# A hybrid decoder trunk on one core: the scan's decays made in two steps, and the last layer's roots moved from GpSimd to ScalarE and VectorE

## The chip, the cores and the metric

One core of a Trainium2 chip runs the whole program. Its engines are TensorE (PE, with its weight loads as PEld), VectorE (DVE), ScalarE (ACT), GpSimd (POOL) and SyncE (SP), each with a queue of its own that it works off in order, and DMA engines that move data between the memories. The metric is the device time of one execution in microseconds: 824.66 us before (the median of three runs, 824.23 to 825.6).

## The reference

Two layers (DEPTH = 2) on 256 tokens of 1024 channels in fp32. Each layer normalises the stream by its root mean square, projects it with one large matrix, and feeds three token mixers: a Mamba-2 state space scan (SSD), sliding-window attention, and forgetting attention. Each mixer's output is gated, projected back to 1024 channels, and merged under sigmoid gates; one more projection is added to the stream. After the second layer a last normalisation gives the output. The two parts that matter here:

```python
def rms_norm(x, w):
    xf = x.astype(jnp.float32)
    y = xf * lax.rsqrt(jnp.mean(xf * xf, axis=-1, keepdims=True) + NORM_EPS)
    return (y * w.astype(jnp.float32)).astype(x.dtype)

# in ssd_chunked_scan: two chunks of 128 tokens, 4 groups of 4 heads
    seg = a_cum[..., :, None] - a_cum[..., None, :]
    decay = jnp.where(causal, jnp.exp(jnp.where(causal, seg, 0.0)), 0.0).astype(dtype)
    cb = jnp.einsum('bclgn,bcsgn->bgcls', cc, bc)
    y_diag = jnp.einsum('bgrcls,bcsgrp->bclgrp', cb[:, :, None] * decay, x_dt)
```

## The kernel before

**Weights and matmuls.** All large products are made with split operands. A weight piece is loaded in fp32 (tile `raw`, 128x1024, queue of SP), ScalarE copies it rounded to `hi`, and VectorE subtracts to get `lo` (function `split`, L286 and L287). PE then multiplies high by high, low by high and high by low into one PSUM bank (`mm`, all matmuls stand at L106, transposes at L110). SP's loads run six pieces ahead, the splits up to four parts ahead of the piece in use.

**What sets the order.** PE's instructions are issued in the order in which the program writes them. A list of operations walks through the weight pieces; between them `pump` enters the steps of generators (`ssd_group`, `swa_quad`, `fox_quad` and others) whose due time has come. A generator says with `yield D_...` how many estimated PE microseconds must pass before its next step. For the other engines a scheduler of the framework chooses the order from the dependencies and from where in the program an instruction was written, so that an instruction written later tends to stand later; `pin` keeps an instruction in the program's order, and `tc.high_priority()` moves one ahead.

**The scan.** `ssd_group(y, g)` makes one group of four heads. Its second step builds for each of the two chunks four decay matrices on VectorE (L829, 128x128 each, `dec`), exponentiates all four in one ScalarE activation (L831), then exponentiates the cumulated sums of the second chunk (L835, `cx`) and multiplies them with C on VectorE (L836). It yields `D_SSD` = 8.0; the next step multiplies the decays with the chunk's products (L848), and after that PE uses them. VectorE and ScalarE work at the same time on the convolution units of the branch: a unit's high and low sums are added by a GpSimd-issued transfer (`dma_sum`, L487), then come an activation (L773), three taps on VectorE (L776), a tanh (L782) and a product (L783).

**The end.** In the last layer `u_out2` and `u_out` make the last projection in three column blocks (256, 512, 256) for each of the two token halves. `out_end` adds the residual (L1133), sums squares (on ScalarE, L242, or for the last block on VectorE, L1137), and for the last block makes the variance, one value per partition, and calls `row_rsqrt2`: GpSimd raises it to the power -0.5 (L253), and two VectorE instructions refine it by a Newton step (L255, L257). Then VectorE scales columns 0 to 639 (L1156), ScalarE the rest (L1158), and SP and ScalarE issue the output transfers (L1157, L1159). Rows with line L1510 are the closing instructions of the program: each engine's DRAIN and the barrier's semaphores, in which GpSimd collects the others.

**The activation table.** Exp, Tanh and Abs run under one table, loaded once at the start beside a 1-wide activation on the tile `tab` (L183).

Of the kernel before, what the change touches and what calls it, by code (L numbers as in the profile page):

```python
# [21 lines left out]
NEG = -1.0e30  # L22
EPS = 1e-6

D_SOFT, D_SOFT2, D_EVAC, D_SSD, D_SSD2 = 7.0, 3.0, 3.0, 8.0, 4.0
D_K, D_Q, D_QK, D_G0, D_FOX, D_BDMA, D_BIAS, D_BC, D_SSD3 = 6.0, 5.5, 2.0, 8.0, 0.0, 4.0, 2.6, 5.5, 1.0
D_GN1, D_GN2, D_CUM, D_H, D_M = 8.0, 13.5, 12.0, (4.8, 6.4), 5.0
BUDGET = 1.35
# [19 lines left out]
def hybrid_trunk(  # L48
# [17 lines left out]
    def T(tag, shape, dtype=F32, bufs=None):  # L66
        count[0] += 1
        return sb.tile(shape, dtype, tag=tag, name=f"{tag}_{count[0]}",
                       bufs=bufs if bufs is not None else BUFS.get(tag, 1))
# [92 lines left out]
    def drain(br):  # L162

        left = 0
        while any(m[2] == br for m in waiting):
            for m in sorted(waiting, key=lambda m: (m[0], m[1])):
                if m[2] == br and allowed(m):
                    left += 1
                    enter(m)
                    break  # L170
            else:
                m = min((m for m in waiting if allowed(m)), key=lambda m: (m[0], m[1]))
                left += 1
                enter(m)
        if left and VERBOSE:
            print("drained", br, left, "at", round(clock["t"], 1))
# [70 lines left out]
        ts(v[:, 0:1], v[:, 0:1], 1.0 / D, EPS, op0=ALU.mult, op1=ALU.add)  # L247
        return v

    def row_rsqrt2(v):  # L250

        r0 = T("sm", [P, 8])
        nc.gpsimd.tensor_tensor(r0[:, 0:1], v, mhalf[:, 0:1], op=ALU.pow)  # L253
        a = T("sm", [P, 8])
        stt(a[:, 0:1], r0[:, 0:1], v, r0[:, 0:1], op0=ALU.mult, op1=ALU.mult)  # L255
        r = T("rs", [P, 8], bufs=4)
        stt(r[:, 0:1], a[:, 0:1], -3.0, r0[:, 0:1], op0=ALU.add, op1=ALU.mult)  # L257
        return r
# [21 lines left out]
    def pin(f):  # L280
        return lambda *a, **k: tc.keep_in_program_order(f(*a, **k))  # L281
# [517 lines left out]
    def ssd_group(y, g):  # L799
        yield lambda: not any(m[2] == 1 for m in waiting)  # L800
        yield "bcg"
        bcg = T("L4", [P, 4, S])
        nc.scalar.dma_start(bcg, y.cumd[4 * g:4 * g + 4, 0, :].partition_broadcast(P))
        yield D_BC
        yield "ssd"
        xdt = T("L2", [P, 2, 256])
        hs = slice(4 * g, 4 * g + 4)
        for t in range(2):
            p = pmx()
            for j in range(2):  # L810
                transpose(p[:, j * P:(j + 1) * P], y.xs[:, 2 * g + j, t * P:(t + 1) * P], ident)
            tt(xdt[:, t, :].rearrange("p (h d) -> p h d", h=4),  # L812
               p[:, 0:256].rearrange("p (h d) -> p h d", h=4), bc(y.dt[:, t, hs], 2, 64), op=ALU.mult)
        p = pmx()
        transpose(p[:, 0:P], y.bcT[:, g, 0:P], ident)
        bt = T("bt", [P, P])
        act(bt, p[:, 0:P], AF.Copy)
        ds = T("ds", [P, 4], bufs=2)
        tt(ds, bcg[:, :, P - 1], y.acum[:, 0, hs], op=ALU.subtract)
        act(ds, ds, AF.Exp)  # L820
        xds = T("L1", [P, 256])
        tt(xds.rearrange("p (h d) -> p h d", h=4), xdt[:, 0, :].rearrange("p (h d) -> p h d", h=4),
           bc(ds, 2, 64), op=ALU.mult)
        decs = []
        for c in range(2):
            tk = slice(c * P, (c + 1) * P)
            dec = T("L2", [P, 4, P])
            for h in range(4):
                stt(dec[:, h, :], bcg[:, h, tk], y.acum[:, c, 4 * g + h:4 * g + h + 1], negtri,  # L829
                    op0=ALU.subtract, op1=ALU.add)  # L830
            act(dec, dec, AF.Exp)  # L831
            decs.append(dec)

        cx = T("L2", [P, 4, P])
        act(cx, bcg[:, :, P:S], AF.Exp)  # L835
        tt(cx, cx, bc(y.bcT[:, 4 + g, P:S], 1, 4), op=ALU.mult)  # L836
        yield D_SSD
        tokens["bcg"] += 1

        p = pmx()  # L840
        mm(p[:, 0:256], bt, xds, start=True, stop=True)
        for c in range(2):
            tk = slice(c * P, (c + 1) * P)
            mm(p[:, 256 + c * P:384 + c * P], y.bcT[:, g, tk], y.bcT[:, 4 + g, tk], start=True, stop=True)
        st = T("st", [P, 256])
        act(st, p[:, 0:256], AF.Copy)
        for c in range(2):
            tt(decs[c], decs[c], bc(p[:, 256 + c * P:384 + c * P], 1, 4), op=ALU.mult)  # L848
        yield Half(D_SSD2)

        py = pmx()
        for c in range(2):
            for j in range(2):
                o = py[:, S * j + P * c:S * j + P * c + P]
                for s in range(c + 1):
                    for i in range(2):
                        h = 2 * j + i
                        hc = slice(64 * h, 64 * h + 64)
                        a, b = (xdt[:, c, hc], decs[c][:, h, :]) if s == 0 else (st[:, hc], cx[:, h, :])
                        mm(o[64 * i:64 * i + 64, :], a, b, start=(s == 0), stop=(s == c))  # L860
        for j in range(2):
            u = 2 * g + j
            stt(y.xs[:, u, :], y.xs[:, u, :], y.dsk[:, u:u + 1], py[:, S * j:S * j + S], op0=ALU.mult, op1=ALU.add)
        yield D_SSD3
        tokens["ssd"] += 1
# [233 lines left out]
    def out_start(y, c, t, i, n):  # L1099
        xo = T("L1" if n == 256 else "L2", [P, n])  # L1100
        xsrc = x2 if y.l == 0 else xres
        nc.scalar.dma_start(xo, xsrc[t * P:(t + 1) * P, c:c + n])
        if i == 0:
            y.ss[t] = T("ss", [P, 4], bufs=4)
            if t == 0:
                y.xn = T("L8", [P, 2, D])
        return xo
# [8 lines left out]
    def u_out2(y, c):  # L1116

        def f(w):
            def late():
                drain(8)  # L1120
                limit(None, True)
            drain(7)
            xo = [out_start(y, c, t, 0, w.n) for t in range(2)]
            none = lambda: None
            for t, p in enumerate(tok2(y.mh, y.ml, w, (none, late, none, none))):
                out_end(y, c, t, 0, w.n, xo[t], p)
            state["pin"] = False
        return f

    def out_end(y, c, t, i, n, xo, p):  # L1130
        sl = slice(c, c + n)
        with tc.high_priority():
            tt(halves(y.xn[:, t, sl]), p, halves(xo), op=ALU.add)  # L1133
            last = y.l + 1 == L
            if last and i == 2:
                junk = T("L2", [P, 512])
                nc.vector.tensor_tensor_reduce(out=junk[:, 0:n], in0=y.xn[:, t, sl], in1=y.xn[:, t, sl],  # L1137
                                               scale=1.0, scalar=0.0, op0=ALU.mult, op1=ALU.add,
                                               accum_out=y.ss[t][:, i:i + 1])
            else:  # L1140
                sum_sq(y.xn, t, c, y.ss[t][:, i:i + 1], n)
            nwb = fin["w"] if last else layers[y.l + 1].nwb
            if i == 2:
                v = y.var[t][:, 1:2]
                pin(stt)(v, y.ss[t][:, 2:3], 1.0 / D, y.var[t][:, 0:1], op0=ALU.mult, op1=ALU.add)
            if last:
                pin(stt)(y.xn[:, t, sl], y.xn[:, t, sl], -0.5, nwb[:, sl], op0=ALU.mult, op1=ALU.mult)
            else:
                nc.scalar.dma_start(xres[t * P:(t + 1) * P, sl], y.xn[:, t, sl])
            if i == 1:  # L1150
                y.var[t] = row_var(y.ss[t], 2)
            if i == 2:
                r = row_rsqrt2(v)
                if last:
                    m = 640
                    ts(y.xn[:, t, 0:m], y.xn[:, t, 0:m], r[:, 0:1], None, op0=ALU.mult)  # L1156
                    nc.sync.dma_start(out2[t * P:(t + 1) * P, 0:m], y.xn[:, t, 0:m])  # L1157
                    act(y.xn[:, t, m:D], y.xn[:, t, m:D], AF.Copy, scale=r[:, 0:1])  # L1158
                    nc.scalar.dma_start(out2[t * P:(t + 1) * P, m:D], y.xn[:, t, m:D])  # L1159
                else:  # L1160
                    h = layers[y.l + 1].h[t] = T("L4", [P, D])
                    for j in range(2):
                        hs = slice(j * 512, (j + 1) * 512)
                        stt(h[:, hs], y.xn[:, t, hs], r[:, 0:1], nwb[:, hs], op0=ALU.mult, op1=ALU.mult)
        if i == 2 and not last:
            launch(5 + t, hT(layers[y.l + 1], t), D_H[t])
        if i == 1:
            pump()
# [345 lines left out]
```

## Time and profile before

| | before |
|---|---|
| median of 3 runs | 824.66 us (824.23 to 825.6) |
| the profiled execution's own time | 825.03 us |
| its span (first to last instruction) | 823.0 us, granted clock 0.996 |
| PE / DVE / ACT / POOL busy | 99% / 81% / 67% / 21% |
| instructions | 15134 |

The profile shows one execution. Busy time counts what an engine executes; a PE row also holds the pipeline behind a matmul, so that small waits of PE are better seen in the starts of two matmuls than in its idle time. Rows of the timeline read: start, duration, engine, line, operation, output<-inputs, shapes, count; in square brackets the idle time before them and who ended it. Rows of windows read: the stretch, its length, then busy time and instruction count of PE, PEld, DVE, ACT and POOL, the granted clock, the DMA share and GB/s. Rows that begin with a line number group the instructions of that line: count, least/median/most nanoseconds, first and last start. An engine's name with a q is its queue: issue, semaphores and DRAINs.

### The profile page before, as it was taken

The page shows a single profiled execution, that of the slowest core. Times are in us where ns is not written, and L with a number is a line of the kernel's source. Part 1 is how long each engine was busy: PE and PEld are TensorE (multiplying, and loading weights), DVE is VectorE, ACT ScalarE, POOL GpSimd, SP SyncE. Part 2 cuts the span into 40 slices and gives each one's busy share as a digit, 9 for nine tenths or more (in the row PEclk, how much of TensorE's full clock was granted, in tenths as well). Part 3 has the DMA queues.
Part 4 walks back from the last instruction along what each step waited for, and adds up shares of the span by engine and source line. Part 5 has one row for each costly group of instructions (what it writes and reads, how often), then busy time and mean ns, then how long its engine had stood idle before and what let it go on. Part 6 is the DMA issues. An engine that isn't in the chain of part 4 may idle for free.

```text
span 823.0 us, 15134 instructions
## 1 busy us (share of the span) xinstructions
PE 811.7 (99%) x5266; PEld 724.5 (88%) x5266; DVE 670.6 (81%) x1466; ACT 550.4 (67%) x1198; POOL 169.9 (21%) x234
## 2 busy tenths in 40 slices
PE   9999999999999999999999999999999999999995
PEld 8998988888888888888999898888889889888895
DVE  6879899799898787965776989988889878787664
ACT  7777778685776768543656777877557767684441
POOL 3066113140310010120006621314002210102100
PEclk9999999999999999999999999999999999999998
DMA  9897869697766554865789777969867555467531
GB/s 312 281 257 189 217 183 266 182 246 226 196 180 186 177 169 151 276 207 194 237 270 259 187 205 200 243 186 259 243 196 212 180 169 166 141 205 264 186 113 64
DMA packets 141653, 170.35 MB, mean 207 GB/s; under 512 B 9314, under 2 KB 110298, under 8 KB 141578
## 3 DMA queue, kind: packets, MB, share of 16 engines
q1 hardware_dynamic: 114960, 140.53, 54.7%
q0 software_dynamic: 12928, 12.63, 9.5%
q10 hardware_dynamic: 13690, 16.24, 6.4%
q8 instruction: 41, 0.67, 0.3%
q14 instruction: 34, 0.28, 0.1%
HBM read 154.63 MB, written 2.16 MB: 191 GB/s over the span
## 4 chain that ended last, share of the span: by engine, by line
PE 90%; DVE 5%; issue 2%; ACT 2%; DMA 1%; POOLq 0%; POOL 0%; SPq 0%; ACTq 0%; DVEq 0%
PE mm L106 78%; PE mx L106 7%; PE mx L110 4%; DVE lo L287 1%; DVE L L776 1%; DVE L L829 1%; ACT hi L286 0%; ACT pp L616 0%; DMA L<-in_x_dram 0%; DMA L<-xres 0%; ACT hi L281 0%; DVE pp L610 0%; DVE L L812 0%; DVE L L727 0%; DVE L L836 0%
## 5 line engine op out<-in xcount | busy, mean ns | idle before, releaser
L287 DVE TENSOR_TENSOR lo<-raw,hi 128x1024 fp32r<-128x1024 f32 (+2 forms) x276 | 311.0, 1145 | 55.8 <-ACT hi L286 54.4
L106 PE MATMUL mm<-L,hi 128*128 128x512 f32 x1056 | 353.2, 386 | 0.0
L106 PE MATMUL mm<-hi,L 128*128 128x512 f32 (+2 forms) x1232 | 323.3, 351 | 0.1
L286 ACT ACTIVATE hi<-raw 128x1024 fp32r<-128x1024 f32 (+2 forms) x276 | 264.7, 983 | 55.3 <-PE mm L106 47.5
L106 PE MATMUL mm<-L,lo 128*128 128x256 f32 x1056 | 266.6, 273 | 0.0
L106 PEld LDWEIGHTS mm<-hi,L 128*128 128x128 f32 x1232 | 216.9, 190 | 24.1 <-issue 1.5
L106 PEld LDWEIGHTS mm<-L,hi 128*128 128x128 f32 x1056 | 194.5, 190 | 26.4 <-issue 3.6
L106 PE MATMUL mm<-lo,L 128*128 128x512 f32 (+2 forms) x616 | 213.8, 349 | 0.8 <-DVE lo L287 0.8
L106 PEld LDWEIGHTS mm<-L,lo 128*128 128x128 f32 x1056 | 202.1, 191 | 5.5
L106 PEld LDWEIGHTS mm<-lo,L 128*128 128x128 f32 x616 | 116.3, 190 | 13.1 <-DVE lo L287 1.6
L487 POOL DMA_DIRECT2D L<-L x68 | 59.5, 930 | 182.2 <-ACT L L486 144.8
L616 ACT ACTIVATE pp<-pp,nm 128x128 f32<-128x128 f32 (+1 forms) x128 | 56.6, 445 | 32.8 <-DVE nm L610 32.8
L994 POOL TENSOR_SCALAR_AFFINE_SELECT bias<-bias 128x128 f32<-128x128 f32 x64 | 31.1, 535 | 98.6 <-DMA bias<-cumd 58.6
L776 DVE SCALAR_TENSOR_TENSOR L<-L,vec,L 128x255 f32<-128x255 f32 (+2 forms) x96 | 46.2, 481 | 1.8
L485 ACT ACTIVATE L<-mm 128x256 f32<-128x256 f32 x84 | 31.8, 378 | 17.0 <-PE mm L106 14.1
L1028 ACT ACTIVATE L<-L 128x512 f32<-128x512 f32 x24 | 15.1, 631 | 32.0 <-DVE L L1025 27.8
L628 DVE TENSOR_SCALAR pp<-pp,rsum 128x128 f32<-128x128 f32 (+1 forms) x128 | 32.5, 320 | 0.5
L487 POOL DMA_DIRECT2D qt<-L x16 | 14.5, 990 | 84.3 <-ACT qt L486 46.5
L880 DVE SCALAR_TENSOR_TENSOR L<-L,L 128x256 f32<-128x256 f32 x48 | 21.2, 446 | 9.4 <-ACT L L879 9.1
L647 ACT ACTIVATE L<-mx 128x512 f32<-128x512 f32 x48 | 26.9, 596 | 1.3 <-PE mx L110 1.3
L879 ACT ACTIVATE L<-L 128x256 f32<-128x256 f32 x48 | 19.9, 414 | 10.8 <-DVE L L478 7.5
L1073 POOL TENSOR_TENSOR L<-L,L 128x512 f32<-128x512 f32 x8 | 12.8, 1599 | 68.3 <-DVE L L1072 68.3
(200 smaller groups left out, 848.2 us busy)
## 6 DMA issues: line engine op xcount, KB each, us to landing
raw<-in_w_in_dram SPq DMA_DIRECT2D x191, 512.0 KB, 4.7
raw<-in_w_proj_dram SPq DMA_DIRECT2D x48, 512.0 KB, 5.5
L<-L POOLq DMA_DIRECT2D x72, 128.0 KB, 5.0
raw<-in_w_out_dram SPq DMA_DIRECT2D x16, 512.0 KB, 4.7
bias<-cumd ACTq DMA_DIRECT2D x16, 256.0 KB, 3.8
L<-cumd ACTq DMA_DIRECT2D x8, 512.0 KB, 5.6
L<-in_gate_bias_dram ACTq DMA_DIRECT2D x12, 256.0 KB, 6.1
qt<-L POOLq DMA_DIRECT2D x16, 128.0 KB, 5.3
```

The source lines that it names most:

```text
L106: nc.tensor.matmul(o, a, b, **kw)
L110: nc.tensor.transpose(o, a, i)
L286: keep(act)(hi, src, AF.Copy)
L287: keep(tt)(lo, src, hi.bitcast(F32), op=ALU.subtract)
L485: act(halves(lo), ordered(p[:, S:2 * S]), AF.Copy)
L487: nc.gpsimd.dma_start(out, lo, accum_op=ALU.add)
L616: act(pp[:, i, sl], pp[:, i, sl], AF.Exp, scale=-1.0, bias=nm[:, e:e + 1], accum_out=sums[:, e:e + 1])
L628: ts(pp[:, i, sl], pp[:, i, sl], rs[:, 2 * i + b:2 * i + b + 1], 0.5, op0=ALU.mult, op1=ALU.mult)
L647: act(pT, pt, AF.Copy)
L776: stt(a[:, s:S], x_[:, 0:S - s], y.vec[:, 16 * j + u:16 * j + u + 1], a[:, s:S], op0=ALU.mult, op1=ALU.add)
L880: stt(o, th, 1.0, o, op0=ALU.add, op1=ALU.mult)
L994: nc.gpsimd.affine_select(out=bias[:, i, dst], in_=bias[:, i, src], compare_op=ALU.is_ge, fill=NEG, base=0, pattern=[[-1, P]], channel_mul ...
```

## The change

It has two independent parts.

The first is in the scan. Between the first chunk's decays and the second chunk's a `yield D_DEC` (2.6) is put in, and `D_SSD` is made 5.4, so that both together are the former 8.0. The second chunk's decays and the product with C are thus written 2.6 estimated PE microseconds later in the program, behind whatever `pump` enters in between.

The second is at the end. In the last layer the root is made by a ScalarE square root and a VectorE reciprocal in place of GpSimd's power; the Newton step stays. The square root needs another activation table, and a 1-wide square root on `tab`, pinned, is written at the start of the last projection, so that the table is loaded there. The first layer keeps the power.

```diff
-D_SOFT, D_SOFT2, D_EVAC, D_SSD, D_SSD2 = 7.0, 3.0, 3.0, 8.0, 4.0
+D_SOFT, D_SOFT2, D_EVAC, D_DEC, D_SSD, D_SSD2 = 7.0, 3.0, 3.0, 2.6, 5.4, 4.0
...
-    def row_rsqrt2(v):
+    def row_rsqrt2(v, last):
 
         r0 = T("sm", [P, 8])
-        nc.gpsimd.tensor_tensor(r0[:, 0:1], v, mhalf[:, 0:1], op=ALU.pow)
+        if last:
+            s = T("sm", [P, 8])
+            act(s[:, 0:1], v, AF.Sqrt)
+            nc.vector.reciprocal(r0[:, 0:1], s[:, 0:1])
+        else:
+            nc.gpsimd.tensor_tensor(r0[:, 0:1], v, mhalf[:, 0:1], op=ALU.pow)
...
         decs = []
         for c in range(2):
+            if c == 1:
+
+                yield D_DEC
             tk = slice(c * P, (c + 1) * P)
...
                 limit(None, True)
             drain(7)
+            if y.l + 1 == L:
+
+                pin(act)(tab, ones[:, 0:1], AF.Sqrt)
             xo = [out_start(y, c, t, 0, w.n) for t in range(2)]
...
-                r = row_rsqrt2(v)
+                r = row_rsqrt2(v, last)
```

The order of PE's and SP's instructions is the same in both kernels. Lines of the new kernel stand 5 to 11 further down. Three places show what moves on the other engines.

VectorE at the first scan group of layer 0 (the same in layer 1). `L_500` is the first chunk's decays, `L_501` (then `L_507`) the second's, `L_502` (then `L_508`) the product with C; `lo_2498` is the low part of a piece that PE is about to use. Before:

```order
L829 SCALAR_TENSOR_TENSOR L_500_2426<-L_471_2310,acum_1725,negtri_79 128x128 x4
L829 SCALAR_TENSOR_TENSOR L_501_2432<-L_471_2310,acum_1725,negtri_79 128x128 x4
L783 SCALAR_TENSOR_TENSOR L_383_1891<-L_506_2463,L_492_2403 128x256
L836 TENSOR_TENSOR L_502_2438<-L_502_2438,L_226_1107 128x512
L287 TENSOR_TENSOR lo_2498<-raw_2269,hi_2497 128x1024
L776 SCALAR_TENSOR_TENSOR L_507_2466<-L_472_2312,vec_893,L_507_2466 128x255
L776 SCALAR_TENSOR_TENSOR L_507_2466<-L_472_2312,vec_893,L_507_2466 128x254
L287 TENSOR_TENSOR lo_2563<-raw_2326,hi_2562 128x1024
```

and with the change:

```order
L837 SCALAR_TENSOR_TENSOR L_500_2426<-L_471_2310,acum_1725,negtri_79 128x128 x4
L837 SCALAR_TENSOR_TENSOR L_507_2464<-L_471_2310,acum_1725,negtri_79 128x128
L788 SCALAR_TENSOR_TENSOR L_383_1891<-L_504_2454,L_492_2403 128x256
L837 SCALAR_TENSOR_TENSOR L_507_2464<-L_471_2310,acum_1725,negtri_79 128x128 x3
L781 SCALAR_TENSOR_TENSOR L_505_2457<-L_472_2312,vec_893,L_505_2457 128x255
L292 TENSOR_TENSOR lo_2498<-raw_2269,hi_2497 128x1024
L781 SCALAR_TENSOR_TENSOR L_505_2457<-L_472_2312,vec_893,L_505_2457 128x254
L844 TENSOR_TENSOR L_508_2470<-L_508_2470,L_226_1107 128x512
L781 SCALAR_TENSOR_TENSOR L_505_2457<-L_472_2312,vec_893,L_505_2457 128x253
L292 TENSOR_TENSOR lo_2563<-raw_2326,hi_2562 128x1024
```

The product with C has moved behind the low part, one tap ahead of it. On ScalarE the activation that feeds the taps (L773, now L778) has moved with them: from behind the three exponentials to behind the first.

ScalarE at the start of the last projection, before:

```order
L281 ACTIVATE hi_9769<-raw_9662 128x1024
L289 ACTIVATE L_1969_9527<-mx_9773 128x512
L281 ACTIVATE L_1969_9527<-mx_9813 128x512
L281 ACTIVATE hi_9820<-raw_9674 128x1024
L281 ACTIVATE hi_9824<-raw_9686 128x1024
```

and with the change:

```order
L286 ACTIVATE hi_9769<-raw_9662 128x1024
L294 ACTIVATE L_1969_9527<-mx_9773 128x512
L286 ACT_TABLE_LOAD
L286 ACTIVATE tab_65<-ones_86 128x1
L286 ACTIVATE L_1969_9527<-mx_9814 128x512
L286 ACTIVATE hi_9821<-raw_9674 128x1024
```

The load and the 1-wide root stand between two copies of transposed columns. No other load follows.

GpSimd's last instructions, before (`L253` is the power, once for each token half):

```order
L1073 TENSOR_TENSOR L_1516_7326<-L_1516_7326,L_1893_9176 128x512
L1073 TENSOR_TENSOR L_1516_7326<-L_1516_7326,L_1917_9263 128x512
L253 TENSOR_TENSOR sm_9938<-sm_9895,mhalf_96 128x1
L253 TENSOR_TENSOR sm_10014<-sm_9979,mhalf_96 128x1
L1510 UNCONDITIONAL_BRANCH
```

and with the change:

```order
L1081 TENSOR_TENSOR L_1516_7326<-L_1516_7326,L_1858_9041 128x512
L1081 TENSOR_TENSOR L_1516_7326<-L_1516_7326,L_1885_9137 128x512
L1081 TENSOR_TENSOR L_1516_7326<-L_1516_7326,L_1893_9176 128x512
L1081 TENSOR_TENSOR L_1516_7326<-L_1516_7326,L_1917_9263 128x512
L1521 UNCONDITIONAL_BRANCH
```

GpSimd's program now ends with an addition of the merge, ahead of the last projection on the other engines.

## The prediction

> **What bounds the kernel now.** I read the busy shares first, then the windows in which the tensor engine is not full, then the timeline of the last microseconds, and last the rows of the program's end.
>
> ```profile
> PE 811.7 (99%) x5266; PEld 724.5 (88%) x5266; DVE 670.6 (81%) x1466; ACT 550.4 (67%) x1198; POOL 169.9 (21%) x234
> 172.00:190.00 18.00, 17.50 (x95) 15.38 (x94) 16.94 (x34) 13.62 (x29) 6.54 (x9) 1.00 0.96 251
> 565.00:582.00 17.00, 16.69 (x91) 14.64 (x90) 16.05 (x32) 12.61 (x27) 7.44 (x9) 1.00 0.93 250
> ```
>
> PE sets the time: 811.7 us busy at full clock. Another engine's order counts only where PE waits for it, or behind PE's last matmul. The change touches two stretches of the first kind (the windows above, the first scan group of each layer, where PE is short of full) and the stretch behind PE. The instruction order shows PE's order unchanged, so PE's work is the same.
>
> At the first scan group PE waits for the low part of a weight piece, and VectorE is late with it because the decays stand ahead:
>
> ```profile
> 182.59 0.59 PE L106 MATMUL mm<-hi,L 128*128 128x512 f32 x2
> 183.68 0.48 PE L106 MATMUL mm<-lo,L 128*128 128x512 f32 x1 [0.50 <-DVE lo L287]
> 179.38 2.18 DVE L829 SCALAR_TENSOR_TENSOR L<-L,acum,negtri 128x128 f32<-128x128 f32 x8
> 181.48 0.41 DVE L783 SCALAR_TENSOR_TENSOR L<-L,L 128x256 f32<-128x256 f32 x1
> 181.82 0.68 DVE L836 TENSOR_TENSOR L<-L,L 128x512 f32<-128x512 f32 x1
> 182.42 1.21 DVE L287 TENSOR_TENSOR lo<-raw,hi 128x1024 fp32r<-128x1024 f32 x1
> 575.06 0.59 PE L106 MATMUL mm<-hi,L 128*128 128x512 f32 x2
> 575.96 0.48 PE L106 MATMUL mm<-lo,L 128*128 128x512 f32 x1 [0.31 <-DVE lo L287]
> 574.08 0.69 DVE L836 TENSOR_TENSOR L<-L,L 128x512 f32<-128x512 f32 x1
> 574.68 1.22 DVE L287 TENSOR_TENSOR lo<-raw,hi 128x1024 fp32r<-128x1024 f32 x1
> ```
>
> Two such matmuls start 0.59 - 0.38 = 0.21 us apart (0.38 is one alone), so the third was due at 183.02 and 575.49 and came at 183.68 and 575.96: 0.66 and 0.47 us lost, 1.13 in all. The modelled idle times (0.50, 0.31) are smaller because a busy row includes the pipeline behind a matmul.
>
> Then the end, in order of time, and the rows of the program's own end (L1510):
>
> ```profile
> 815.52 0.16 DVE L281 SCALAR_TENSOR_TENSOR sm<-ss,sm 128x1 f32<-128x1 f32 x1
> 815.60 0.42 DVE L281 SCALAR_TENSOR_TENSOR L<-L,nwb 128x256 f32<-128x256 f32 x1
> 815.76 0.67 POOL L253 TENSOR_TENSOR sm<-sm,mhalf 128x1 f32<-128x1 f32 x1 [7.16 <-DVE sm L281]
> 816.47 0.22 DVE L255 SCALAR_TENSOR_TENSOR sm<-sm,sm 128x1 f32<-128x1 f32 x1 [0.45 <-POOL sm L253]
> 816.91 0.62 ACT L1158 ACTIVATE L<-L,rs 128x384 f32<-128x384 f32 x1 [3.54 <-DVE rs L257]
> L1510 SPq DRAIN  x2: 7/7/7, 820.4 to 820.5; - x2
> L1510 POOLq EVENT_SEMAPHORE  x2: 17/17/17, 822.3 to 822.4; - x2
> L1510 POOLq DRAIN  x1: 6512/6512/6512, 815.7 to 815.7; - x1
> ```
>
> This is what matters most. SP has seen the last output land and drains at 820.4 to 820.5. GpSimd, which takes part in the closing barrier, issued a DRAIN at 815.7, right beside its last instruction (the power at 815.76), and that DRAIN lasts 6.51 us, to 822.2. Only then, at 822.3, does the barrier go on, and the span ends at 823.0. So the last 1.8 us wait for GpSimd, not for the output. The chain of waits does not name this: it stops at the output's last scaling.
>
> **The change part by part.**
>
> *GpSimd's power leaves the end.* After it GpSimd's last instruction is its last addition for the merge:
>
> ```profile
> 762.00 2.13 POOL L1073 TENSOR_TENSOR L<-L,L 128x512 f32<-128x512 f32 x1 [4.60 <-DVE L L1072]
> ```
>
> It ends at 764.1; a DRAIN of the same 6.5 us behind it would be over at 770.6, under PE's matmuls. The barrier then waits for SP at 820.5 in place of 822.3: -1.8 us less a hop of some 0.04, so **-1.75**. Bounds: 0, if the DRAIN's length does not come from the power (a rival below), and -1.8, since SP is next.
>
> [...]
>
> *The root itself.* The variance is ready at 815.52 + 0.16 = 815.68 and L255 starts at 816.47: the power costs 0.79 us with its hops. Now a ScalarE square root of 128x1 and a VectorE reciprocal stand there. Nearest rows: a 128x1 activation, and reciprocals of 128x4.
>
> ```profile
> 1.46 1.28 ACT L183 ACT_TABLE_LOAD   x1 [1.46 <-PEq L1503]
> 2.75 0.20 ACT L183 ACTIVATE tab<-tab 128x1 f32<-128x1 f32 x1
> L625 DVE RECIPROCAL rsum<-sums x32: 169/177/180, 72.7 to 690.7; 128x4 f32<-128x4 f32 x32
> ```
>
> 815.68 + 0.03 + 0.20 + 0.03 + 0.18 + 0.03 = 816.15; VectorE's 128x256 row (815.60, to 816.02) may hold the reciprocal back until 816.02, then L255 starts at 816.23. A hop between engines is 0.03 to 0.04 (the power ends at 815.76 + 0.67 = 816.43, L255 follows at 816.47). I take the middle, 816.19: **-0.28**. Bounds: -0.32, and +0.05 if both take twice the row. The waits added queue nothing new: behind the root on ScalarE stands the scaling that needs it, behind the reciprocal L255. The other token half's root, at 808, has PE's matmuls over it.
>
> *The table load.* It is issued behind the activation at 792.84, into a gap of ScalarE:
>
> ```profile
> 792.84 0.60 ACT L289 ACTIVATE L<-mx 128x512 fp32r<-128x512 f32 x1 [3.43 <-PE mx L110]
> 795.96 0.60 ACT L281 ACTIVATE L<-mx 128x512 fp32r<-128x512 f32 x1 [2.52 <-PE mx L110]
> 797.34 0.19 PEld L106 LDWEIGHTS mm<-hi,L 128*128 128x128 f32 x1 [0.16 <-DVE L L281]
> ```
>
> 1.28 + 0.20 = 1.48 us against an idle 2.52: **0**. The cover is PE's transposes, due at 795.9. It must be covered: at 797.34 PE already waits 0.16 us for what follows from the activation at 795.96, so whatever the load took beyond 2.52 would lengthen PE's wait one for one. No second load appears in the order; the copies, squares and roots behind it run under the loaded table.
>
> [...]
>
> *The decays in two steps.* The same instructions run, in another order: in both first groups L783 stands between the second chunk's decays, the product L836 goes behind the late low part, and the first tap (L776) of the next convolution unit comes ahead of it. So the low part gains L836 (0.60, from 181.82 to 182.42) and pays a tap, which itself needs ScalarE's L773 (now second behind the first exponential) and, before that, the landing of GpSimd's adding transfer:
>
> ```profile
> 181.08 0.61 ACT L835 ACTIVATE L<-L 128x512 f32<-128x512 f32 x1
> 182.13 0.59 ACT L773 ACTIVATE L<-L,vec 128x256 f32<-128x256 f32 x1
> 176.16 0.85 POOL L487 DMA_DIRECT2D L<-L  x1
> DMA to landing us min/median/max: 5.3/5.3/5.3
> 573.36 0.61 ACT L835 ACTIVATE L<-L 128x512 f32<-128x512 f32 x1
> 568.05 0.87 POOL L487 DMA_DIRECT2D L<-L  x1
> DMA to landing us min/median/max: 5.2/5.2/5.2
> L776 DVE SCALAR_TENSOR_TENSOR L<-L,vec,L 128x255 f32<-128x255 f32 (+2 forms) x96 | 46.2, 481 | 1.8
> ```
>
> A tap holds VectorE between 0.34 (L783, nearly the same shape, start to start) and 0.48 (its mean duration); I take 0.40. Layer 0: the add lands at 176.16 + 5.3 = 181.46, later than ScalarE is free (181.08), so L773 runs to 182.05, the tap starts at 182.09 (VectorE is free at 181.82) and the low part at 182.49 in place of 182.42: +0.07. Layer 1: the add has landed at 573.25, L773 starts at 573.36 and ends at 573.95, the tap runs from 574.08, the low part starts at 574.48 in place of 574.68: -0.20. Sum **-0.13**, which PE passes on, as nothing but PE stands behind. Bounds: -1.13 (both stalls gone), +0.3 if the landings vary by some tenths. The other groups' reordering I cost at nothing:
>
> ```profile
> 190.00:565.00 375.00, 374.72 (x2461) 334.72 (x2460) 307.68 (x681) 252.27 (x554) 74.31 (x97) 1.00 0.72 209
> 582.00:795.00 213.00, 213.00 (x1297) 187.92 (x1296) 169.81 (x361) 131.22 (x261) 26.72 (x36) 1.00 0.62 192
> ```
>
> There PE is full (the second number of a row against the first) while VectorE has a fifth to spare, so a split or product some tenths later is covered by PE's work in hand; with that cover gone, each tenth would cost a tenth.
>
> **Sum:** -1.75 - 0.28 - 0.13 = -2.16 us. The profiled execution took 825.03 us round a span of 823.0, 0.37 above the median of 824.66; its span should become 820.8 and it 822.9. From the median that is **822.5**.
>
> **The rivals.**
>
> *The end does not move* (the DRAIN belongs to the program's end and not to the power, or waits for something else that ends at 822.2). For it: the trace has no second long DRAIN beside which to lay it. Against: it was issued at 815.7, with the power, and SP had nothing left to do after 820.5. Time: only the root and the decays, -0.41, so 824.25. Chance 0.13. [...]
>
> *The low part comes at once* in both first groups (taps ready, order luckier than I have it): the decays bring 1.13 in place of 0.13, 821.5. For it: 1.13 us is all that PE loses there. Against: the tap now stands ahead of the split. Chance 0.10.
>
> *The tap waits for the add and holds the low part.* Before, two more ScalarE activations (181.08 to 182.13) covered the landing. The adding transfers between 160 and 186 landed after (least, median, most):
>
> ```profile
> DMA to landing us min/median/max: 4.9/5.7/7.2
> ```
>
> At 7.2 in both layers the adds land at 183.36 and 575.25, the low parts start 0.59 + 0.04 + 0.40 later, 184.39 and 576.28, against 182.42 and 574.68: +1.97 and +1.60. With the end's -2.03 that is +1.5, 826.2, slower. It decides against the whole gain from 2.03 us on, which is both adds landing above 6.4. Against: in the profile they took 5.3 and 5.2, and GpSimd's order is the same. Chance 0.05.
>
> **How the numbers follow.** My forecast has 0.72: 822.5, and with bounds of some tenths on root and decays 821.9 to 823.2. Rivals 0.13, 0.10, 0.05. The range of all reaches from the lucky decays to the unmoved end: 821.5 to 824.4. About 0.2%, 1.65 us, is what a measurement can tell from none: faster by more holds most of the forecast (0.60 of its 0.72, as 2.16 is only half a microsecond above) and the lucky decays, 0.69; slower 0.05; within, the rest, 0.26.
>
> **What would show it.** Right: GpSimd's DRAIN early and hidden, its barrier event 0.05 behind SP's DRAIN, the step that was L255 starting some 0.5 us behind the variance, the table load between 793.4 and 795, PE's two waits near 0.7 and 0.3. Wrong: a GpSimd DRAIN that still ends some 2 us behind SP's; a ScalarE activation at 796 that waits for the load; PE's wait for the low part above 1 us at 183 or 575.

## The result and the profile after

The changed kernel takes **830.16 us** (median of 6 runs, 828.62 to 831.12) beside 824.46 us for the kernel before on the same chip (6 runs): a ratio of 1.0054, 95% interval 1.0043 to 1.0066. It is slower, by 4.5 us as the ratio has it and by 5.7 us between the medians. The forecast was 822.5 us, 821.5 to 824.4: the sign was wrong. The execution that left the profile took 831.12 us round a span of 829.3 us, the longest of the six, so single microseconds in it are read with care.

**The end came as forecast.** The closing rows of the kernel after, and the last rows before the output's scaling (the columns are those of the same rows before):

```profile
L1521 POOLq EVENT_SEMAPHORE  x4: 17/17/17, 828.6 to 829.2; - x4
L1521 POOLq DRAIN  x3: 46/93/7954, 770.4 to 829.1; - x3
L1521 SPq DRAIN  x3: 7/7/7, 828.5 to 828.8; - x3
...
823.94 0.16 DVE L286 SCALAR_TENSOR_TENSOR sm<-ss,sm 128x1 f32<-128x1 f32 x1
824.14 0.20 ACT L255 ACTIVATE sm<-sm 128x1 f32<-128x1 f32 x1 [2.35 <-DVE sm L286]
824.37 0.17 DVE L256 RECIPROCAL sm<-sm 128x1 f32<-128x1 f32 x1
824.57 0.22 DVE L260 SCALAR_TENSOR_TENSOR sm<-sm,sm 128x1 f32<-128x1 f32 x1
```

GpSimd's long DRAIN (7954 ns, the first of the three in its row) starts at 770.4 and is over at 778.4, under PE's matmuls. The barrier follows SP's DRAIN at 828.5 within a tenth. The root takes from 824.10 (variance ready) to 824.57. Between the end of PE's last matmul and the end of the span lay 8.44 us before (814.56 to 823.0) and lie 6.31 us now (822.99 to 829.3): 2.1 us are gone from the end.

**The loss is PE's.** What PE waits for in the kernel after (engine, line, releaser: total, times, longest), and behind it the same for the kernel before:

```profile
PE mx L106 <- DVE L L856: 4.1, 2, 2.9
PE mm L106 <- DVE lo L292: 1.6, 2, 1.4
```

```profile
PE mm L106 <- DVE lo L287: 0.8, 2, 0.5
```

A wait is there that was not there before: twice, once in each layer, PE waits for L856, VectorE's product of decays and scores (L848 before). PE's matmuls are the same 5266 in the same order, so the start of each can be laid beside its start before; the difference is called PE's lag here. It grows at the first scan groups: by 0.9 us at the low part at 183.68 (before's time) and 1.3 us at 190.8 in layer 0; by 2.94 us at 583.08 and 1.4 us over the matmuls just behind in layer 1. Another 1.4 us stand at 167.7, behind a broadcast that was 8.5 us on its way; the change moves nothing ahead of it, and no other profile here has a step there. Some 1.0 us lies further ahead still, where the change moves nothing either, and some 0.5 us is made up in between. At PE's last matmul the lag is 8.4 us; less the 2.1 us of the end, that is the span's 6.3 us.

**Why the product is late.** In layer 1, ScalarE's rows of the kernel before and then of the kernel after. ACTq is ScalarE's sequencer, which issues transfers; `L<-cumd` is the broadcast of one group's cumulated sums to all partitions (512 KB), which `ssd_group` issues in its first step:

```profile
573.88 0.62 ACT L831 ACTIVATE L<-L 128x512 f32<-128x512 f32 x1
574.00 0.37 ACTq L803 DMA_DIRECT2D L<-cumd  x1
575.42 2.00 ACT L286 ACTIVATE hi<-raw 128x1024 fp32r<-128x1024 f32 x2
578.44 0.42 ACT L782 ACTIVATE L<-L 128x256 f32<-128x256 f32 x1 [1.02 <-DVE L L776]
```

```profile
578.26 0.61 ACT L843 ACTIVATE L<-L 128x512 f32<-128x512 f32 x1
579.83 2.00 ACT L291 ACTIVATE hi<-raw 128x1024 fp32r<-128x1024 f32 x2
581.57 0.37 ACTq L808 DMA_DIRECT2D L<-cumd  x1
581.72 0.41 ACT L787 ACTIVATE L<-L 128x256 f32<-128x256 f32 x1
```

and VectorE's, before and after:

```profile
580.33 0.15 DVE L819 TENSOR_TENSOR ds<-L,acum 128x4 f32<-128x4 f32 x1
581.03 1.28 DVE L848 TENSOR_TENSOR L<-L,mx 128x512 f32<-128x512 f32 x2 [0.54 <-ACT st L846]
```

```profile
583.92 0.68 DVE L1077 SCALAR_TENSOR_TENSOR L<-L,mm 128x512 f32<-128x512 f32 x1
589.31 0.16 DVE L824 TENSOR_TENSOR ds<-L,acum 128x4 f32<-128x4 f32 x1 [4.71 <-DMA L<-cumd]
589.39 1.28 DVE L856 TENSOR_TENSOR L<-L,mx 128x512 f32<-128x512 f32 x2
```

with PE's use of the first product, before and after:

```profile
583.08 0.88 PE L106 MATMUL mx<-L,L 128*64 128x128 f32 x12
583.78 0.39 PE L106 MATMUL mx<-L,st 128*64 128x128 f32 x4
```

```profile
590.12 1.55 PE L106 MATMUL mx<-L,L 128*64 128x128 f32 x12 [2.87 <-DVE L L856]
591.46 0.64 PE L106 MATMUL mx<-L,st 128*64 128x128 f32 x4
```

Before, the sequencer had run ahead of ScalarE's work: the third group's broadcast went out at 574.00, while five activations that stand ahead of it in the queue were still to come, and 4.4 us before the tanh of the convolution unit (L782). After, that broadcast stands one place later, behind the tanh. The tanh waits for VectorE's taps, the sequencer stops at that wait, and the broadcast goes out at 581.57, with the tanh. ScalarE's queue there, in the order in which the program issues it, before and after:

```
L803 DMA L_1527_7386<-cumd_6543 128x4x256
L782 ACTIVATE L_1513_7313<-L_1502_7272 128x256
L1021 DMA L_1535_7428<-in_gate_bias_dram 128x512
```

```
L787 ACTIVATE L_1513_7313<-L_1500_7263 128x256
L808 DMA L_1527_7386<-cumd_6543 128x4x256
L1029 DMA L_1535_7428<-in_gate_bias_dram 128x512
```

The split delays the broadcast in a second way, too. The tag of its tile (`L4`) has two buffers, so the third group's broadcast overwrites the first group's, whose last reader on ScalarE is `cx` (L835, then L843). Before, it left 0.03 us behind the end of `cx` (573.36 + 0.61 = 573.97). After, `cx` ends at 578.87, which is 0.8 us later by PE's time (578.87 less PE's lag of 4.10); from there to 581.57, for 2.7 us, it is the tanh that holds the broadcast up. In run 3 below, where the broadcast stands ahead of the tanh, it again leaves 0.03 us behind `cx` (575.86 + 0.61 = 576.47).

The third group needs nothing of the broadcast for long. But its `ds`, four columns on VectorE, reads the broadcast and stands in VectorE's queue just ahead of the *first* group's products, which PE wants at once. VectorE stands idle for 4.71 us with those products behind a waiting 0.16 us instruction. The numbers close: PE's lag ahead of this place is 4.10 us, so the products' start at 589.39 is 585.29 in before's time, 4.26 us later than 581.03. Before, the first of them was ready at 581.71 (0.68 us for one, as run 6 below shows them apart) and PE used it at 583.08, 1.37 us of slack. 4.26 - 1.37 is 2.89, and PE lost 2.94.

### The profile page after: what moved, and what is told of

It is laid out like the page before. It is cut to its first block, busy times and chain, and to the rows that moved or that the text cites. A ratio compares the mean times of both kernels' runs of the same rounds, so it can differ in the third digit from the quotient of the medians.

```text
span 829.3 us, 15137 instructions
## 1 busy us (share of the span) xinstructions
PE 813.9 (98%) x5266; PEld 726.3 (88%) x5266; DVE 671.6 (81%) x1468; ACT 552.0 (67%) x1202; POOL 172.1 (21%) x232
## 4 chain that ended last, share of the span: by engine, by line
PE 79%; ACT 7%; DMA 6%; DVE 5%; issue 2%; POOL 0%; SPq 0%; ACTq 0%; DVEq 0%; POOLq 0%
PE mm L106 69%; PE mx L106 7%; DMA L<-cumd 3%; PE mx L110 3%; ACT hi L291 2%; DVE lo L292 2%; DMA L<-L 1%; ACT pp L621 1%; DVE L L781 1%; ACT L L778 1%; ACT L L490 1%; POOL bias L1002 0%; DMA bias<-cumd 0%; ACT L L491 0%; DMA L<-in_x_dram 0%
## 5 line engine op out<-in xcount | busy, mean ns | idle before, releaser
L1002 POOL TENSOR_SCALAR_AFFINE_SELECT bias<-bias 128x128 f32<-128x128 f32 x64 | 33.0, 553 | 96.5 <-DMA bias<-cumd 55.6
L923 POOL TENSOR_TENSOR sm<-sm,mhalf 128x4 f32<-128x4 f32 x8 | 8.1, 1020 | 90.3 <-DVE sm L920 90.3
```

The lines of the kernel that those rows point to most:

```text
L1002: nc.gpsimd.affine_select(out=bias[:, i, dst], in_=bias[:, i, src], compare_op=ALU.is_ge, fill=NEG, base=0, pattern=[[-1, P]], channel_mul ...
```

## The experiments

Each run is compared with runs of the kernel before on the same chip, whose medians lay between 825.5 and 825.9 us; ratios are against these. Line numbers shift by a few from kernel to kernel.

**1 and 2: the two halves apart.** The first has the two-step decays alone, with `D_DEC` and `D_SSD` as in the change; the second the end alone, with the early table load.

> The split of the decays alone; the root stays POOL's power as before. Theory (the third group's broadcast is issued behind the tanh on ScalarE's queue, its ds holds VectorE, the products of decay and score come late, PE waits): all of the loss and none of the gain at the end, so 824.5 + (5.7 + 2.1) = 832.3 us, 831 to 833; VectorE's ds waits some 15 to 17 us in all for the broadcast (6.8 before), and the matrix product waits 2 to 3 us for VectorE's product (L850 here) in layer 1. Rival (the loss comes from the end or from the table load): no change, 824.5.

> The root on ScalarE and VectorE with the early table load alone; the decays are made in one step as before. Theory: the end is shorter by what the profile after showed, 8.44 to 6.31 us behind the last matmul, so 824.5 - 2.1 = 822.4 us, 822.0 to 822.8. Rival (the end doesn't move in the median): 824.5.

The scan's half: 831.39 us, ratio 1.0068 (1.0054 to 1.0081), +5.6 us. The end's half: 823.29 us, ratio 0.9971 (0.9959 to 0.9983), -2.4 us. The waits of the scan's half:

```profile
PE mx L106 <- DVE L L850: 3.4, 2, 2.8
DVE ds L819 <- DMA L<-cumd: 13.8, 6, 4.7
```

So the loss is the scan's, the gain the end's, and the new wait comes with the scan's half.

**3: the same split, with the broadcast early.**

```diff
-        nc.scalar.dma_start(bcg, y.cumd[4 * g:4 * g + 4, 0, :].partition_broadcast(P))
+        with tc.high_priority():
+            nc.scalar.dma_start(bcg, y.cumd[4 * g:4 * g + 4, 0, :].partition_broadcast(P))
```

> The split of the decays alone, with the broadcast given a high priority, so that it stands ahead of the tanh on ScalarE's queue again (and ahead of two evictions more than before); TensorE's order is the same. Theory: VectorE's ds waits as before (some 7 us in all), the matrix product's wait for VectorE's product is gone, and the time comes back to within 1 us of before: 824.0 to 825.5 (about 1 us of layer 0's late low part may stay). Rival (the loss comes from the decays themselves being made later, or from the other rows that moved): the loss stays, 830 to 833.

825.82 us, ratio 0.9997 (0.9987 to 1.0007). The whole loss is gone, though the decays are made in two steps as in run 1. ScalarE's sequencer and VectorE in layer 1, and VectorE's wait:

```profile
576.50 0.37 ACTq L804 DMA_DIRECT2D L<-cumd  x1
...
582.16 0.16 DVE L820 TENSOR_TENSOR ds<-L,acum 128x4 f32<-128x4 f32 x1
582.24 1.28 DVE L851 TENSOR_TENSOR L<-L,mx 128x512 f32<-128x512 f32 x2
...
DVE ds L820 <- DMA L<-cumd: 7.1, 5, 2.8
```

Neither `ds` nor the products wait there any more. The rival "the decays themselves, or the other rows that moved" falls, to within the interval of 0.1%. The edit is in every group's broadcast, so the fourth group's moves as well; the next run moves less.

**4: the same split and the late broadcast, with `ds` out of the way.** The framework is told to issue the third group's `ds` behind the first group's second product. On VectorE one instruction per layer moves, by two places; on ScalarE the exponential that reads it moves by one; nothing else.

```diff
-        tt(ds, bcg[:, :, P - 1], y.acum[:, 0, hs], op=ALU.subtract)
+        with tc.issue_after(ld[y.l, g - 2]) if g == 2 else ExitStack():
+            tt(ds, bcg[:, :, P - 1], y.acum[:, 0, hs], op=ALU.subtract)
...
-            tt(decs[c], decs[c], bc(p[:, 256 + c * P:384 + c * P], 1, 4), op=ALU.mult)
+            ld[y.l, g] = tt(decs[c], decs[c], bc(p[:, 256 + c * P:384 + c * P], 1, 4), op=ALU.mult).ins
```

> The split of the decays alone, and the third group's broadcast late as in the changed kernel; only its ds on VectorE is put behind the first group's two products of decay and score, where it holds nothing that PE waits for at once. Theory (the harm is not the late landing but the instruction that waits for it at the head of VectorE's queue): the matrix product's wait for VectorE's product is gone though the broadcast lands just as late, and most of the loss comes back: 824.5 to 827. Rival (the late landing itself does it, through something else that needs the broadcast): the loss stays, 830 to 833.

826.66 us, ratio 1.0004 (0.9995 to 1.0013). In layer 1:

```profile
579.67 0.37 ACTq L803 DMA_DIRECT2D L<-cumd  x1
...
582.62 1.27 DVE L851 TENSOR_TENSOR L<-L,mx 128x512 f32<-128x512 f32 x2
587.20 0.16 DVE L820 TENSOR_TENSOR ds<-L,acum 128x4 f32<-128x4 f32 x1 [3.31 <-DMA L<-cumd]
```

The broadcast is as late as in run 1 (579.67 here, 580.32 there), and VectorE still idles 3.31 us for it. But now it idles with the products done, and PE does not notice. It is the place of the waiting instruction in VectorE's queue that costs, not the wait.

**5 and 6: the harm without the change.** The kernel before, with the third group's broadcast put behind the tanh. The framework then places `ds` behind both products by itself; in run 6 a high priority for `ds` puts it between the two.

```diff
+        with tc.issue_after(tanh[-1]) if g == 2 else ExitStack():
+            nc.scalar.dma_start(bcg, y.cumd[4 * g:4 * g + 4, 0, :].partition_broadcast(P))
...
+        with tc.high_priority() if g == 2 else ExitStack():
+            tt(ds, bcg[:, :, P - 1], y.acum[:, 0, hs], op=ALU.subtract)
```

(The last two lines in run 6 alone; `tanh` is the list of the units' tanh instructions.)

> No part of the change: the kernel before, with the third group's broadcast put behind the conv unit's tanh on ScalarE's queue; the order then has its ds behind the first group's two products of decay and score on VectorE. Theory (a late landing alone is harmless while nothing that is wanted at once stands behind its reader): within 1 us of before, 825 to 826.5. Rival (the late landing itself makes the loss): 829 to 832.

> No part of the change: the kernel before, with the same late broadcast, and its ds standing between the first group's two products on VectorE, so that the second product waits behind it. Theory (a waiting ds at the head of VectorE's queue holds a product that PE wants): the loss appears without any split, some 1 to 3 us a layer: 827 to 831, and PE's wait for VectorE's product (L850 here) is back. Rival (the loss needs the split): as the run without the ds between, 825 to 826.5.

Run 5: 826.68 us, ratio 1.0013 (1.0004 to 1.0022), a tenth or two of a microsecond above what was expected, though the broadcast in layer 1 leaves at 578.94, with the tanh. Run 6: 833.03 us, ratio 1.0086 (1.0069 to 1.0104). Its rows in layer 1, and PE's waits:

```profile
590.99 0.16 DVE L821 TENSOR_TENSOR ds<-L,acum 128x4 f32<-128x4 f32 x1 [4.20 <-DMA L<-cumd]
591.07 0.68 DVE L850 TENSOR_TENSOR L<-L,mx 128x512 f32<-128x512 f32 x1
...
591.80 0.44 PE L106 MATMUL mx<-L,L 128*64 128x128 f32 x4 [2.29 <-DVE L L850]
...
PE mx L106 <- DVE L L850: 4.6, 2, 2.3
```

The loss appears with no split at all, from one instruction's place in the queue. It is larger than expected (7 us, not 1 to 5): the two stalls are 4.6 us, and PE's clock fell to 0.50 behind both, of which more below.

**7: the end, with a power that nobody reads.** The end's half, and beside the new root the old power on GpSimd into a spare column.

```diff
             nc.vector.reciprocal(r0[:, 0:1], s[:, 0:1])
+            nc.gpsimd.tensor_tensor(s[:, 1:2], v, mhalf[:, 0:1], op=ALU.pow)
```

> The root on ScalarE and VectorE with the early table load, and beside it the power on POOL as before, into a column that nobody reads. Nothing on the way of the numbers is added. Theory (POOL's DRAIN ends some 5.8 us behind POOL's last operation, and sets the end): the span goes back to about that of before, its POOL DRAIN ending last, and the time to 825.0 to 825.8 against 825.6. Rival (the end was shortened by the root's shorter way): the gain stays, 823.3.

825.65 us, ratio 0.9998 (0.9989 to 1.0006): the gain is gone. GpSimd's last operation and the closing rows:

```profile
817.71 0.67 POOL L257 TENSOR_TENSOR sm<-sm,mhalf 128x1 f32<-128x1 f32 x1 [7.17 <-DVE sm L287]
...
L1519 POOLq EVENT_SEMAPHORE  x4: 17/17/17, 824.2 to 824.9; - x4
L1519 POOLq DRAIN  x3: 46/98/6512, 817.7 to 824.7; - x3
L1519 SPq DRAIN  x3: 7/7/7, 822.1 to 824.4; - x3
```

SP first drains at 822.1, the barrier moves at 824.2, when the DRAIN that started at 817.7 is over. Since nothing reads this power, the time is the DRAIN's and not the root's.

**8: the whole change with the broadcast early.** The edit of run 3, in the changed kernel.

> The whole change, with the broadcast given a high priority as in the third run. Theory: the split costs and brings nothing once the broadcast is early, and the end's gain stays: 825.6 - 2.3 = 823.3 us, 822.7 to 824.0. Rival (split and end do not add up): above 825.

824.57 us, ratio 0.9983 (0.9972 to 0.9993): faster than before, above the 822.7 to 824.0 expected, and a microsecond short of the end's half alone. VectorE's low parts and PE's waits for them show a place where it may be:

```profile
183.41 1.22 DVE L292 TENSOR_TENSOR lo<-raw,hi 128x1024 fp32r<-128x1024 f32 x1
...
576.13 1.22 DVE L292 TENSOR_TENSOR lo<-raw,hi 128x1024 fp32r<-128x1024 f32 x1
...
184.69 0.48 PE L106 MATMUL mm<-lo,L 128*128 128x512 f32 x1 [0.73 <-DVE lo L292]
...
577.41 0.48 PE L106 MATMUL mm<-lo,L 128*128 128x512 f32 x1 [0.50 <-DVE lo L292]
```

The low part that PE waits for starts 0.99 and 1.45 us later than before (182.42 and 574.68), each 0.2 us more than PE's lag there (0.78 and 1.25), and the lag grows by 0.22 and 0.20 us at these two places. One profile says little of this: in the six with the split (the change, runs 1, 3, 4, 8 and 9) the two places together cost PE 0.4 to 1.5 us more than in the profile of before, 0.9 on average; in the six without it (runs 2, 5, 6, 7, 10 and 11) the cost lies between 0.3 us less and 0.4 us more, 0.0 on average. So in the profiles the split costs some 0.9 us even where its own transfer does no harm. The times do not show this microsecond: run 3 by itself shows no loss, and run 11 below, the end's half with early broadcasts and no split, has nearly the same ratio as this run. That it is real is likely, not shown.

**9: the change again.**

> The changed kernel once more, beside the runs of its parts, to see whether the parts add up. The split alone came to a ratio of 1.0068 and the end alone to 0.9971, so their sum would be 1.0039 [1.0021, 1.0057]; the first comparison of the change gave 1.0054 [1.0043, 1.0066]. Theory (the parts add): 1.0035 to 1.0055, 828.8 to 830.5 us. Rival (the parts hinder each other by another microsecond): above 1.006.

829.25 us, ratio 1.0043 (1.0028 to 1.0058). The halves add up.

**10 and 11: two variants of the end's half.** Run 10 leaves out the early 1-wide square root; the table is then loaded with the first token half's root. Run 11 gives the broadcasts a high priority, without the split.

> The end's half without the square root of one column that fetches the table ahead of the output; the load then comes with the first token half's root. Theory (the load of 1.28 us lies under PE's last products there, and the second half's root needs none): as with it, 823.3 us, 822.7 to 824.0. Rival (the load delays what the first half's way gates): 824 to 825.

> The end's half alone, with the broadcasts given a high priority. Theory (in the order of before no broadcast is late, so an earlier one brings nothing): as the end's half alone, 823.3 us, 822.7 to 824.0. Rival (the 0.5 to 0.8 us that PE and ds still wait around the scan are the broadcast's): 822 to 822.6, which would be the fastest of all.

823.15 us, ratio 0.9967 (0.9955 to 0.9978), and 823.91 us, ratio 0.998 (0.9969 to 0.999). The early load buys nothing, and an earlier broadcast buys nothing where none is late. The end's half, with or without the early load, beats both kernels.

## Why the prediction was wrong, step by step

**GpSimd's DRAIN, -1.75: right.** Runs 2 and 7 show both directions. The end shrank by 2.1 us in the profile, of which the root is 0.32. One detail differed: I put the end of the DRAIN 6.5 us behind the end of the last addition, and it came 5.8 us behind it; as the DRAIN is issued beside the start of that operation, it lasted 7.95 us. In the profiles of before, after and runs 1, 7 and 8 it ends 5.8 us behind the end of GpSimd's last operation (816.43 to 822.2 before, 772.54 to 778.4 after). It lasts 6.51 us beside a power of 0.67 us (before, runs 1 and 7) and 7.95 us beside an addition of 2.12 us (after, run 8).

**The root, -0.28: right.** 0.79 us before, 0.47 us after, so -0.32.

**The table load, 0: right.** The kernel after:

```profile
801.88 1.28 ACT L286 ACT_TABLE_LOAD   x1
803.18 0.20 ACT L286 ACTIVATE tab<-ones 128x1 f32<-128x1 f32 x1
804.38 0.60 ACT L286 ACTIVATE L<-mx 128x512 fp32r<-128x512 f32 x1 [1.00 <-PE mx L110]
```

The 1-wide activation starts 0.02 us behind the load's end, and the next one still waits 1.00 us for PE, not for the load.

**The decays in two steps, -0.13: wrong by sign and by far** (+5.6 us in run 1), in two places.

The step that failed is the sentence "The other groups' reordering I cost at nothing", with the reason that PE is full there and that "a split or product some tenths later is covered by PE's work in hand". I had followed VectorE's arithmetic and ScalarE's activations, and had not followed the transfer that moved with them: ScalarE's queue also issues the third group's broadcast, and the order showed it one place later, behind the tanh. One place was not some tenths but some 3.5 us by PE's time (581.57 less PE's lag of 4.10 is 577.47, against 574.00): 2.7 us because the place is behind a semaphore wait, and 0.8 us because `cx`, whose end the broadcast waits for, is itself made later. The landing took longer, too: 7.7 us, from 581.57 to the `ds` at 589.31, against at most 6.3 us before (574.00 to 580.33, where `ds` did not wait); why is not shown. Who reads it, and what stands behind the reader on VectorE, I did not ask. The slack that this had to fit into was 1.37 us, and the rows that give it were in the trace of before.

The low part by itself was mis-sized: -0.13 forecast, some +0.9 on average in the profiles with the split. In the kernel after, PE's lag there changed by +0.92 in layer 0, where +0.07 was forecast, and by -0.09 in layer 1, where -0.20 was. The rival "the tap waits for the add and holds the low part" names the mechanism in layer 0: in the kernel after, ScalarE's activation waited 0.94 us for the adding transfer, the first tap came 0.84 us after VectorE was free, and the low part behind it.

```profile
184.64 0.60 ACT L778 ACTIVATE L<-L,vec 128x256 f32<-128x256 f32 x1 [0.94 <-DMA L<-L]
185.28 0.48 DVE L781 SCALAR_TENSOR_TENSOR L<-L,vec,L 128x255 f32<-128x255 f32 x1 [0.84 <-ACT L L778]
185.68 1.22 DVE L292 TENSOR_TENSOR lo<-raw,hi 128x1024 fp32r<-128x1024 f32 x1
```

It was given 0.05 and a price of 3.6 us for both layers; the profile shows 0.9 us of PE's lag, in layer 0 alone. One of my signs of being wrong came with it: PE's wait for the low part there was 1.4 us, above the 1 us that I had named.

**The chances.** Slower had 0.05, all of it in that one rival. (The 0.60 and 0.10 of "faster" make 0.70, not the 0.69 that I gave it.) None of the rivals was "a transfer moves behind a wait", though the order of ScalarE's queue, from which I took the activations, has that row.

## What to carry to other kernels

When a change moves instructions, follow each transfer that an engine's queue issues: ask which wait it now stands behind, whose buffer it overwrites, who reads what it brings, and what stands behind that reader in the reader's own queue. A late transfer whose reader holds up nothing costs nothing that the times show (run 4, ratio 1.0004); the same transfer costs microseconds when a tiny instruction that needs it stands ahead of work that another engine wants now (run 6, 7 us). And at the end of a program, look at which engine the closing barrier waits for (here GpSimd's DRAIN held it until 5.8 us behind GpSimd's last operation): the end's half of this change, kept alone, is the faster kernel.

## What the runs showed of the hardware that was not expected

**A stall can cost more than its length.** PE's clock in two stretches of the kernel after, behind its stall of 2.87 us in layer 1, and in one of run 1 behind a stall of 2.82 us (the granted clock is the number behind the five engines' busy times):

```profile
589.00:591.00 2.00, 0.88 (x8) 0.88 (x10) 1.67 (x4) 1.50 (x3) 0.00 (x0) 0.67 0.51 199
591.00:593.00 2.00, 2.00 (x21) 1.67 (x17) 2.00 (x3) 2.00 (x3) 0.00 (x0) 0.50 0.04 10
```

```profile
589.00:591.00 2.00, 2.00 (x27) 1.59 (x26) 1.98 (x3) 2.00 (x3) 0.00 (x0) 1.00 0.09 31
```

In the first, four 128x128 matmuls take 0.64 us and not 0.39, and 1.4 us more are lost before the clock is back; in the second the clock stays full after nearly the same stall. Run 9 has it too (0.50 behind a stall of 2.77 us in layer 1), and run 6 in both layers, behind stalls of 2.3 us. There the clock falls only after PE has resumed, in layer 0 at 195.32:

```profile
195.00:197.00 2.00, 1.68 (x19) 1.45 (x20) 2.00 (x3) 2.00 (x3) 0.00 (x0) 0.96 0.01 4
197.00:199.00 2.00, 2.00 (x6) 1.58 (x5) 2.00 (x3) 0.75 (x1) 0.00 (x0) 0.50 0.73 166
```

In each of these four cases the trace has the clock at half for 3.4 us (3.41 in the first, 589.67 to 593.08), and PE lost 1.4 to 1.8 us beyond the stall. Of two stalls of nearly the same length (2.87 and 2.82 us) only one was followed by it, and stalls of 2.3 us were, so the length of the stall alone does not decide it here; what does is not shown.

**An issuing queue runs ahead of its engine, until a wait.** Before, a transfer left ScalarE's queue at 574.00, while five activations ahead of it ran until 577.4. After, it stood behind the tanh, whose wait ended with VectorE's last tap at 581.4, and it left at 581.57. So its place behind five activations cost it nothing, and its place behind an open wait cost it the rest of that wait, 2.7 us.
